# Four modulation-weight loads in another pool, and the scale and shift of turned norms on two engines

## The chip, the cores and the metric

The kernel runs on one core of one Trainium2 chip. A core has five engines with instruction queues of their own: TensorE (PE, with a separate queue row PEld for the loading of the stationary operand), VectorE (DVE), ScalarE (ACT), GpSimd (POOL) and SyncE (SP), which here only issues DMA transfers. The metric is the device time of one execution in microseconds (us). Three runs of the kernel before gave 1665.51, 1665.57 and 1665.77 us.

## What is computed

Two transformer blocks on 256 tokens of width 1024, each with two layers, all in fp32. The change lies in the first block. Cut to what matters, one of its layers is

```python
sh1, sc1, g1, sh2, sc2, g2 = adaln(c, w_mod[l], b_mod[l])      # silu(c) @ w_mod + b_mod, six parts of 1024
h = modulate(rms_norm(x, norm1_g[l]), sh1, sc1)                # h * (1 + scale) + shift
q, k, v, up, ca, cb = project_inputs(h, w_in[l], ...)
attn = diff_attn_post(diff_attention(q, k_all, v_all, lam), subln_g[l], lambda_init)
mix = concatenate([attn, pool_mixer(up), conformer_conv(ca, cb)])
x = x + g1 * (mix @ w_out[l])
x = x + g2 * swiglu(modulate(rms_norm(x, norm2_g[l]), sh2, sc2), w_ffn_in[l], w_ffn_out[l])
```

In layer 0 a second stream of 256 tokens (ctx) goes through the same steps beside x, with its own modulation; in layer 1 only x does. `diff_attention` has 4 heads with two softmaxes each, of which the second is subtracted from the first.

## The kernel before, in words

Tokens lie in four tiles t of 128 (t = 0, 1 are x, t = 2, 3 are ctx). Every product of weights is made of three fp32r products of high and low parts: the weights come by DMA into a tile `raw` (or `wm`), L202 (ScalarE) casts the high part, L204 (VectorE) subtracts it to get the low part, and L156 issues the matmuls. Work is written as Python generators that are woven together; a scheduler then sets the order of each engine's queue, and a tile's first write waits until the last readers of the tile that had its place before are done. So which pool a tile comes from changes when its load may start, and with that the order that the scheduler gives.

The pools that matter: `A8` (12 places of 8 KB per partition, activations), `hl` (4 places of 8 KB, split weights), and in PSUM `acc` (4 banks), `aux` (3 banks) and `ob` (1 bank). All loads are issued by SP, and `dma` (L148) chains them, so that SP issues them in program order: a load that waits for its place holds up every load behind it.

Attention of layer 0 runs at about 130 to 235 us. `front` (L1297 to L1304) makes two score matmuls of 64 rows into two `acc` banks (tile `acc` in the queue's rows), takes the maximum (L1297, VectorE), its negative (L1298), the exponential with its sum (L1299, ScalarE, which frees the bank), and combines the two halves (L1302 to L1304). For t = 0, 1 there are 512 keys, for t = 2, 3 there are 256. `back` turns the result (L248, `transpose4`, into `aux`), copies it (L1313, ScalarE) and multiplies it with the values into `ob`; `norm` (L1323 to L1329) scales, and `turn` (L1334, L1335) writes the operand of the output projection, whose matmuls are the first `acc<-hl,a` rows with 512 columns behind the attention.

Woven into it at two steps per step is `side()`: mixing and convolution, and then `ada_rows` for parts 2, 3 and 4 of the modulation: per part and half n two loads of 1 MB (`wm`, 12 loads in all) and eight matmuls of 32 rows by 512 columns per bank (`aux<-wm,csf`, 4 of them per load, each two records in the trace), then a copy (L341). Part 2 goes to the gates (L391), parts 3 and 4 to columns (matmuls with 2 columns, `aux<-km,s` 128x2, and L368).

The norms ahead of a layer's projections: `half_square` (L409), `halves_rstd` (L421, L422, GpSimd), the scaling in `norm_front` (L443, VectorE), and `norm_back`: four transposes into one `aux` bank, per column j one ScalarE activation with the tile's scale and shift (L461), the cast of the high part (L462, ScalarE) and the difference (L463, VectorE). It runs with scale and shift 10 times: for four tokens' tiles behind the output projection of layer 0 (266 to 293 us), for four ahead of layer 1 (653 to 680 us) and for two behind the output projection of layer 1 (797 to 820 us). Each time takes 8 columns, so L461 has 80 instructions.

Of the kernel before, what the change touches and what calls it, by code (L numbers as in the profile page):

```python
# [9 lines left out]
F32 = mybir.dt.float32  # L10
# [3 lines left out]
AF = mybir.ActivationFunctionType  # L14
ALU = mybir.AluOpType
# [4 lines left out]
P = 128  # L20
# [77 lines left out]
class _Kernel:  # L98
# [227 lines left out]
            k = k0 + j  # L326
            self.mm(o[j * GROUP:(j + 1) * GROUP, :], self.csf[:, k, :], raw[:, j, :], start=(k < 4), stop=(k >= 4))

    def ada_rows(self, l, part):
        out = []  # L330
        for n in range(2):
            c0 = part * D + n * 512
            b = self.bank()
            for k0 in range(0, KD, 4):
                raw = self.whl.tile([P, 4, 512], F32, tag="hl", name=self.nm("wm_"))
                self.dma(raw, self.wview(self.io["w_mod"][l], k0, 4, c0, c0 + 512))
                self.ada_products(b, k0, raw)
                if k0 == 0:
                    yield
            r = self.S2([P, 512])  # L340
            self.nc.vector.tensor_copy(r, b)  # L341
            out.append(r)
            yield
        self._rows = out
# [101 lines left out]
    def norm_back(self, x, t, G, S, out, halves=(0, 1)):  # L446

        nc = self.nc
        i = t * P
        for h in halves:  # L450
            b = self.transpose4([x[:, (4 * h + j) * P:(4 * h + j + 1) * P] for j in range(4)])
            hi, lo = (out[q][h][:, :, i:i + P] for q in range(2))
            tmp = self.S2([P, 4, P])
            if S is None:
                g = G(t)[:, 4 * h:4 * h + 4]
                nc.vector.tensor_mul(tmp, b, g.unsqueeze(2).to_broadcast([P, 4, P]))
            else:
                for j in range(4):
                    k = 4 * h + j
                    g, s = G(t)[:, k:k + 1], S(t)[:, k:k + 1]  # L460
                    nc.scalar.activation(tmp[:, j, :], b[:, j, :], AF.Identity, scale=g, bias=s)  # L461
            nc.scalar.copy(hi, tmp)  # L462
            nc.vector.tensor_sub(lo, tmp, hi.bitcast(F32))  # L463

# [487 lines left out]
    def layer1(self, l, S, xin, hT, first=()):  # L952

        nc, io = self.nc, self.io
# [16 lines left out]
        def band_load():  # L971
            band = self.A8([P, 2, 4, SEQ])
            for kt in range(2):
                self.dma(band[:, kt], io["k_band"][kt].rearrange("p (g t) -> p g t", g=4))
            return band
# [38 lines left out]
        def add(gts):  # L1014
            last = [None]

            def evac(t, n, b):
                cs = slice(n * 512, (n + 1) * 512)
                tmp = self.S2([P, 512])
                with self.behind(last[0]):  # L1020
                    nc.vector.tensor_mul(tmp, b, gts[t // 2][:, cs])
                r = res[t // 2][:, t % 2, cs]
                last[0] = nc.vector.tensor_add(r, r, tmp)  # L1023
                return last[0]
            return evac

        hT2 = None
        if not last:
            gates = [self.gate(l, 2, s) for s in streams]

            band, pp = band_load(), pool_pieces()

            def side():
                for s in streams:
                    for _ in self.pool_mix(S, stat, s, band, mB, pp):
                        next(conv, None)
                        yield
                mA.extend(self.parts(TQ))
                for _ in conv:
                    yield  # L1040
                yield from self.ada_rows(l, 2)
                self.rows_to_gates(gates)
                for p, d in ((3, 2), (4, 3)):
                    yield from self.ada_rows(l, p)
                    self.rows_to_cols(S.mod[:, d], S.part(p))

            rf = lambda t: res[t // 2][:, t % 2, :]
            out = self.out_proj(mstat, io["w_out"][l], TQ, add(gates), lambda t: done(t))

            def side_all():  # L1050
                yield from side()
                while not self.fronts:
                    yield
                for _ in range(2):
                    next(out)
                    yield

            self.weave(self.diff_attention(S, qT, kT, v, rq, q_toks, mA, LAG), side_all(), 2.0)
            for s, name in enumerate(("x", "ctx")):
                res[s] = self.reload(name)  # L1060
            G2, S2 = self.modulation(S, l, 1, "n2")
            hT2 = self.norm_out(512)
            done = self.norm_step(rf, G2, S2, hT2)
            for _ in out:
                pass
            g2, nxt = [None, None], []

            def side2():
                yield
                yield  # L1070
                for s in streams:
                    g2[s] = self.gate(l, 5, s)
                nxt.append(self.setup1(l + 1))
                yield from self.ada_sums(l, 5, streams)
                self.sums_to_gates(g2)
                nx = nxt[0]
                nx.rest()
                yield from self.setup2()
                self.gate_next = self.gate(l + 1, 2, 2)
                for p, d, st in ((0, 0, [0, 1]), (1, 1, [0, 1]), (3, 2, [0]), (4, 3, [0])):  # L1080
                    yield from self.ada_sums(l + 1, p, st)
                    self.sums_to_cols(nx.mod[:, d], nx.part(p))
                yield from self.ada_sums(l + 1, 2, [0])
                self.sums_to_gates([self.gate_next])

            end = {}

            def done_ffn(t):
                if t == 0:
                    end["hT"] = self.norm_out(512)  # L1090
                    end["step"] = self.norm_step(rf, *self.modulation(nxt[0], l + 1, 0, "n1"), end["hT"])
                end["step"](t)

            self.weave(
                self.ffn_wide(hT2, io["w_ffn_in"][l], io["w_ffn_out"][l], self.glu(512), add(g2), done_ffn),
                side2(), 0.85)
            return nxt[0], res[0], end["hT"]
# [24 lines left out]
        bias, nxt, end = [], [], {}  # L1122
# [687 lines left out]
```

## Time and profile before

| | before |
|---|---|
| median of 3 runs | 1665.57 us (1665.51 to 1665.77) |
| profiled execution | 1667.61 us |
| its span | 1665.8 us |
| mean granted TensorE clock | 0.983 |
| PE busy | 1618.0 us (97%) |
| DVE busy | 1180.4 us (71%) |
| ACT busy | 793.9 us (48%) |
| POOL busy | 43.8 us (3%) |

The span is what the trace covers; 1.8 us lie around it. The profiled execution took 2.04 us longer than the median. Busy shares are means over stages with different limits. The granted clock is given as a share of full speed: 1.00 is 2.4 GHz and 0.50 is 1.2 GHz, and a value between them is a mixture within the stretch.

### The profile page before, as it was taken

How to read it: one execution, taken by the hardware profiler on the slowest of the kernel's cores; microseconds unless marked ns; L12 is line 12 of the kernel's file. 1: busy time of each engine (PE TensorE's matmuls, PEld its weight loads, DVE VectorE, ACT ScalarE, POOL GpSimd, SP SyncE). 2: the span in 40 equal slices, each digit the busy share in tenths (PEclk: the TensorE clock that was granted, in tenths of full speed). 3: DMA queues.
4: the chain of work that ended last, by engine and by line, in shares of the span. 5: the costliest groups of instructions: out<-in, count | busy, mean ns of one | idle time of the engine just before them, and what ended most of it. 6: DMA issues, size and time to landing. Idle time of an engine off the chain costs nothing.

```text
span 1665.8 us, 24269 instructions
## 1 busy us (share of the span) xinstructions
PE 1618.0 (97%) x9241; PEld 1354.8 (81%) x9241; DVE 1180.4 (71%) x2130; ACT 793.9 (48%) x1347; POOL 43.8 (3%) x99
## 2 busy tenths in 40 slices
PE   7999999999999999999799899999999999999999
PEld 5787568878888888886698899767999987689998
DVE  4796656856575555986566457877887888778786
ACT  4334436323222224655543346765555577665554
POOL 1000000000000000000000001000000010000000
PEclk8999979999999999999899999999999999999999
DMA  9421651745375553432369655432656554246553
GB/s 329 129 89 59 245 177 55 225 148 168 108 228 174 175 153 113 140 114 82 99 224 243 194 188 159 151 102 88 204 181 190 177 150 150 87 128 189 189 181 122
DMA packets 183011, 262.71 MB, mean 158 GB/s; under 512 B 11277, under 2 KB 122864, under 8 KB 182896
## 3 DMA queue, kind: packets, MB, share of 16 engines
q1 hardware_dynamic: 182616, 260.85, 50.1%
q8 instruction: 72, 1.18, 0.3%
q10 hardware_dynamic: 280, 0.33, 0.2%
q14 instruction: 43, 0.35, 0.1%
HBM read 259.84 MB, written 1.31 MB: 157 GB/s over the span
## 4 chain that ended last, share of the span: by engine, by line
PE 69%; DVE 12%; issue 8%; DMA 6%; ACT 3%; POOL 1%; SPq 0%; POOLq 0%; ACTq 0%; DVEq 0%
PE aux L156 34%; PE acc L156 27%; PE ob L156 6%; DVE hl L204 3%; DMA raw<-in_w_mod_dram 3%; PE aux L248 2%; DVE a L1236 2%; DVE s L1236 1%; ACT hl L202 1%; DMA a<-dbias 1%; DMA raw<-in_w_ffn_out_dram 1%; DVE s L355 1%; DMA raw<-in_w_in_dram 1%; ACT s L461 1%; DVE sm L843 1%
## 5 line engine op out<-in xcount | busy, mean ns | idle before, releaser
L156 PE MATMUL acc<-hl,a 128*128 128x512 f32 (+3 forms) x3072 | 720.4, 387 | 8.1 <-ACT hl L202 2.9
L156 PEld LDWEIGHTS acc<-hl,a 128*128 128x128 f32 x3072 | 553.5, 190 | 127.2 <-issue 15.5
L202 ACT CAST hl<-raw 128x1024 fp32r<-128x1024 f32 (+2 forms) x382 | 393.6, 1036 | 473.5 <-PE aux L156 141.4
L156 PE MATMUL aux<-a,hl 128*128 128x256 f32 (+1 forms) x4032 | 578.5, 304 | 8.1 <-ACT a L462 2.9
L156 PEld LDWEIGHTS aux<-a,hl 128*128 128x128 f32 x4032 | 539.4, 192 | 41.5 <-ACT a L462 3.7
L204 DVE TENSOR_TENSOR hl<-raw,hl 128x1024 fp32r<-128x1024 f32 (+2 forms) x382 | 457.8, 1203 | 162.0 <-ACT hl L202 160.3
L355 DVE SCALAR_TENSOR_TENSOR s<-raw,csf,s 128x1024 f32<-128x1024 f32 x70 | 88.7, 1281 | 46.8 <-DMA raw<-in_w_mod_dram 46.7
L248 PEld LDWEIGHTS aux<-km,s 128*128 128x128 f32 (+1 forms) x384 | 45.2, 143 | 35.9 <-issue 20.1
L248 PE MATMUL aux<-km,s 128*128 128x128 f32 (+1 forms) x384 | 60.0, 284 | 12.3 <-DVE s L443 8.0
L156 PE MATMUL ob<-a,hl 128*128 128x512 f32 (+1 forms) x288 | 64.3, 372 | 0.0
L156 PEld LDWEIGHTS ob<-a,hl 128*128 128x128 f32 x288 | 51.2, 188 | 9.4
L524 ACT ACTIVATE s<-aux 128x512 f32<-128x512 f32 x33 | 19.7, 598 | 66.0 <-PE aux L156 66.0
L552 ACT ACTIVATE s<-s,c2a,c2b 128x256 f32<-128x256 f32 x88 | 48.0, 593 | 5.9 <-DVE s L549 5.9
L527 ACT CAST a<-s 128x512 fp32r<-128x512 f32 x33 | 20.4, 618 | 54.9 <-DVE s L526 54.8
L549 DVE TENSOR_TENSOR s<-aux,km 128x512 f32<-128x512 f32 x44 | 30.4, 691 | 20.5 <-PE aux L156 20.5
L1236 DVE SCALAR_TENSOR_TENSOR a<-up,c,a 128x512 f32<-128x512 f32 x60 | 43.5, 748 | 0.5
L525 DVE SCALAR_TENSOR_TENSOR s<-s,aux 128x512 f32<-128x512 f32 x33 | 22.6, 685 | 29.4 <-ACT s L524 29.4
L248 PE MATMUL aux<-km,a 128*128 128x128 f32 (+1 forms) x196 | 31.1, 289 | 10.5 <-ACT a L770 7.9
L409 ACT ACTIVATE jk<-a 128x512 bf16<-128x512 f32 x44 | 28.1, 640 | 25.2 <-DVE a L1023 19.7
L553 DVE SCALAR_TENSOR_TENSOR s<-s,c2a,s 128x255 f32<-128x255 f32 x88 | 38.7, 479 | 1.4 <-ACT s L552 1.4
L248 PEld LDWEIGHTS aux<-km,a 128*128 128x128 f32 (+1 forms) x196 | 23.7, 146 | 18.6 <-ACT a L770 8.1
L555 DVE SCALAR_TENSOR_TENSOR s<-s,c2b,s 128x255 f32<-128x255 f32 x88 | 38.7, 480 | 0.1
(257 smaller groups left out, 1364.3 us busy)
## 6 DMA issues: line engine op xcount, KB each, us to landing
raw<-in_w_ffn_in_dram SPq DMA_DIRECT2D x88, 512.0 KB
raw<-in_w_up_dram SPq DMA_DIRECT2D x88, 512.0 KB
raw<-in_w_in_dram SPq DMA_DIRECT2D x60, 512.0 KB
raw<-in_w_mod_dram SPq DMA_DIRECT2D x56, 512.0 KB
raw<-in_w_ffn_out_dram SPq DMA_DIRECT2D x44, 512.0 KB
raw<-in_w_down_dram SPq DMA_DIRECT2D x44, 512.0 KB
wm<-in_w_mod_dram SPq DMA_DIRECT2D x16, 1024.0 KB
raw<-in_w_out_dram SPq DMA_DIRECT2D x32, 512.0 KB
```

The source lines that it names most:

```text
L156: self.nc.tensor.matmul(o, lhsT, rhs, start=start, stop=stop)
L202: nc.scalar.copy(hl[:, 0, :n], raw[:, :n])
L204: nc.vector.tensor_sub(hl[:, 1, :n], raw[:, :n], hl[:, 0, :n].bitcast(F32))
L248: self.nc.tensor.transpose(b[:rows, j * P:(j + 1) * P], s, self.ident)
L355: self.nc.vector.scalar_tensor_tensor(accs[s], raw, c, accs[s], op0=ALU.mult, op1=ALU.add)
L409: self.nc.scalar.activation(junk, x[:, h * 512:(h + 1) * 512], AF.Square, scale=D ** -0.5, accum_out=ss[:, h:h + 1])
L525: nc.vector.scalar_tensor_tensor(th, th, 1.0, g, op0=ALU.add, op1=ALU.mult)
L549: nc.vector.tensor_mul(y, x.rearrange("p (j t) -> p j t", j=2), R2)
L552: nc.scalar.activation(o[:, j, :], y[:, j, :], AF.Identity, scale=wc(1, ff), bias=bc(ff))
L553: nc.vector.scalar_tensor_tensor(o[:, j, 1:SEQ], y[:, j, 0:SEQ - 1], wc(0, ff), o[:, j, 1:SEQ], op0=ALU.mult, op1=ALU.add)
L555: nc.vector.scalar_tensor_tensor(o[:, j, 0:SEQ - 1], y[:, j, 1:SEQ], wc(2, ff), o[:, j, 0:SEQ - 1], op0=ALU.mult, op1=ALU.add)
L1236: nc.vector.scalar_tensor_tensor(o, up[:, ct, :, k:k + SEQ], w, o, op0=ALU.mult, op1=ALU.add)
```

## The change

Two edits. In `ada_rows`, the two loads of half n = 1 of parts 2 and 3 of layer 0 take their places in `A8` and no longer in `hl`. In `norm_back`, the columns with odd j go to VectorE as one `tensor_scalar` (multiply by the scale, add the shift) that reads the same PSUM bank.

```diff
-    def ada_rows(self, l, part):
+    def ada_rows(self, l, part, more=False):
+
         out = []
         for n in range(2):
             c0 = part * D + n * 512
             b = self.bank()
             for k0 in range(0, KD, 4):
-                raw = self.whl.tile([P, 4, 512], F32, tag="hl", name=self.nm("wm_"))
+                if more and n:
+                    raw = self.A8([P, 4, 512])
+                else:
+                    raw = self.whl.tile([P, 4, 512], F32, tag="hl", name=self.nm("wm_"))
                 self.dma(raw, self.wview(self.io["w_mod"][l], k0, 4, c0, c0 + 512))
...
                     g, s = G(t)[:, k:k + 1], S(t)[:, k:k + 1]
-                    nc.scalar.activation(tmp[:, j, :], b[:, j, :], AF.Identity, scale=g, bias=s)
+                    if j % 2:
+                        nc.vector.tensor_scalar(tmp[:, j, :], b[:, j, :], g, s, op0=ALU.mult, op1=ALU.add)
+                    else:
+                        nc.scalar.activation(tmp[:, j, :], b[:, j, :], AF.Identity, scale=g, bias=s)
             nc.scalar.copy(hi, tmp)
             nc.vector.tensor_sub(lo, tmp, hi.bitcast(F32))
...
-                yield from self.ada_rows(l, 2)
+                yield from self.ada_rows(l, 2, True)
                 self.rows_to_gates(gates)
                 for p, d in ((3, 2), (4, 3)):
-                    yield from self.ada_rows(l, p)
+                    yield from self.ada_rows(l, p, p == 3)
                     self.rows_to_cols(S.mod[:, d], S.part(p))
```

SP's queue has the same 541 rows in the same order; four of the 12 `wm` loads have another destination. The scheduler gives the other engines another order in the attention. Lines behind the first edit have numbers higher by 4 in the changed kernel, and those behind the second by 7 (L461 is L468, and the new VectorE instruction is L466).

Place 1, TensorE in the attention of layer 0, where fronts of t = 2 (`acc_1658` to `acc_1774`, 64 rows, a pair each) stand beside modulation products (`aux_1638`, from the loads `wm_1639` and `wm_1645`). Before:

```order
L156 MATMUL acc_1607<-a_95_619,a_94_618 128x512
L156 MATMUL acc_1612<-a_95_619,a_94_618 128x512
L248 MATMUL aux_1620<-km,s_241_1537 128x128 x4
L248 MATMUL aux_1627<-km,s_235_1511 128x128 x4
L156 MATMUL aux_1638<-wm_1639,csf 32x512
L156 MATMUL ob_1574<-a_145_995,s_271_1632 128x128 x4
L156 MATMUL aux_1638<-wm_1639,csf 32x512 x3
L156 MATMUL aux_1638<-wm_1645,csf 32x512 x4
L156 MATMUL acc_1658<-a_95_619,a_94_618 128x256
L156 MATMUL acc_1663<-a_95_619,a_94_618 128x256
```

And in the changed kernel:

```order
L248 MATMUL aux_1627<-km,s_235_1511 128x128 x4
L156 MATMUL acc_1658<-a_95_619,a_94_618 128x256
L156 MATMUL acc_1663<-a_95_619,a_94_618 128x256
L156 MATMUL ob_1574<-a_145_995,s_271_1632 128x128 x4
L156 MATMUL acc_1713<-a_95_619,a_94_618 128x256
L156 MATMUL acc_1718<-a_95_619,a_94_618 128x256
L156 MATMUL acc_1769<-a_95_619,a_94_618 128x256
L156 MATMUL acc_1774<-a_95_619,a_94_618 128x256
L156 MATMUL aux_1638<-a_273_1639,csf 32x512 x4
L248 MATMUL aux_1671<-km,s_251_1560 128x128 x4
```

The three pairs `acc_1658`, `acc_1713` and `acc_1769` now stand together, ahead of the products of `aux_1638`, which before stood ahead of the first of them.

Place 2, VectorE in the changed kernel, some 20 instructions later in the same stage (L345 copies modulation rows, L395 adds to the gates, L372 adds to the columns, L1304 is the maximum of a front):

```order
L395 TENSOR_TENSOR gate_1161<-gate_1161,aux_1691 128x512
L345 COPY s_292_1707<-aux_1694 128x512
L1331 TENSOR_TENSOR s_302_1738<-ob_1574,sm_1739 128x512
L1334 TENSOR_REDUCE sm_1740<-s_301_1737 128x4
L372 TENSOR_TENSOR mod_535<-aux_1790,cb_590 128x8
L1304 TENSOR_REDUCE sm_1765<-acc_1769 128x1
L1336 TENSOR_TENSOR s_302_1738<-s_302_1738,sm_1746 128x512
L1305 SCALAR_TENSOR_TENSOR sm_1766<-sm_1765,rq_620 128x1
L1304 TENSOR_REDUCE sm_1765<-acc_1774 128x1
```

The maxima of the pair `acc_1769`, `acc_1774`, whose matmuls moved ahead, still stand behind L372, which needs matmuls (`aux_1790`) that come 18 rows later on TensorE.

Place 3, VectorE in the changed kernel at the norm behind the output projection of layer 1, second tile of tokens (L447 is the scaling, L466 the new instruction, `s_1094` and `s_1096` the two halves of 512):

```order
L447 TENSOR_SCALAR s_1087_6494<-a_400_2082,sm_6501 128x512 x2
L204 TENSOR_TENSOR hl_6599<-raw_6597,hl_6599 128x1024
L204 TENSOR_TENSOR hl_6628<-raw_6626,hl_6628 128x1024
L466 TENSOR_SCALAR s_1094_6511<-aux_6506,G_5998,S_5999 128x128
L466 TENSOR_SCALAR s_1096_6523<-aux_6518,G_5998,S_5999 128x128
L466 TENSOR_SCALAR s_1094_6511<-aux_6506,G_5998,S_5999 128x128
L466 TENSOR_SCALAR s_1096_6523<-aux_6518,G_5998,S_5999 128x128
L470 TENSOR_TENSOR a_1062_6367<-s_1094_6511,a_1061_6366 128x4x128
```

Two low parts of weights (L204) now stand between the scaling and the first odd column, and the columns of the two halves alternate, where on ScalarE the four columns of one half stood ahead of those of the other.

## Rows read from the trace of the kernel before

**Rows 1.** The page: busy time of each engine, and the chain that ended last.

```profile
PE 1618.0 (97%) x9241; PEld 1354.8 (81%) x9241; DVE 1180.4 (71%) x2130; ACT 793.9 (48%) x1347; POOL 43.8 (3%) x99
...
PE 69%; DVE 12%; issue 8%; DMA 6%; ACT 3%; POOL 1%; SPq 0%; POOLq 0%; ACTq 0%; DVEq 0%
```

**Rows 2.** Windows of the attention: length, busy of PE, PEld, DVE, ACT, POOL, clock, DMA, GB/s.

```profile
130.00:140.00 10.00, 8.19 (x32) 5.11 (x31) 9.89 (x19) 5.31 (x10) 0.00 (x0) 0.83 0.33 105
...
156.00:160.00 4.00, 4.00 (x23) 4.00 (x23) 2.05 (x8) 0.25 (x1) 1.22 (x2) 0.57 0.00 0
160.00:188.00 28.00, 27.98 (x170) 18.21 (x171) 18.35 (x44) 18.04 (x40) 1.52 (x3) 1.00 0.44 151
188.00:214.00 26.00, 25.23 (x164) 12.53 (x157) 15.95 (x52) 8.30 (x25) 1.20 (x2) 1.00 0.92 332
214.00:230.00 16.00, 12.98 (x44) 7.80 (x45) 8.74 (x26) 6.24 (x16) 1.20 (x2) 0.52 0.53 184
230.00:235.00 5.00, 5.00 (x17) 4.23 (x16) 3.85 (x13) 4.50 (x11) 0.00 (x0) 0.50 0.00 0
```

**Rows 3.** Waits of PE, then of SP's queue, 130 to 240 and 100 to 240.

```profile
PE aux L248 <- DVE s L1329: 2.0, 1, 2.0
PE acc L156 <- ACT s L1299: 1.7, 2, 1.0
...
SPq L148 <- PE aux L156: 31.3, 8, 12.9
```

**Rows 4.** Timeline of PE: start, duration, instruction, records, and idle time before.

```profile
184.05 1.09 PE L248 MATMUL aux<-km,s 128*128 128x128 f32 x8
185.08 1.04 PE L156 MATMUL aux<-wm,csf 128*32 128x512 f32 x2
186.05 1.16 PE L156 MATMUL ob<-a,s 128*128 128x128 f32 x8
187.14 1.92 PE L156 MATMUL aux<-wm,csf 128*32 128x512 f32 x14
188.99 0.70 PE L156 MATMUL acc<-a,a 64*128 64x256 f32 x4
...
214.38 1.03 PE L156 MATMUL acc<-a,a 64*128 64x256 f32 x2 [0.96 <-ACT s L1299]
...
226.00 1.22 PE L156 MATMUL ob<-a,s 128*128 128x128 f32 x4 [0.62 <-ACT s L1313]
...
230.44 3.33 PE L156 MATMUL acc<-hl,a 128*128 128x512 f32 x7
```

**Rows 5.** Timelines of ACT and DVE: the exponentials and maxima of fronts, and L368.

```profile
187.27 0.78 ACT L1299 ACTIVATE s<-acc,sm,rq 128x512 f32<-128x512 f32 x1 [0.46 <-DVE sm L1298]
...
190.85 0.57 ACT L1299 ACTIVATE s<-acc,sm,rq 128x256 f32<-128x256 f32 x1
...
186.43 0.74 DVE L1304 SCALAR_TENSOR_TENSOR s<-s,sm 128x512 f32<-128x512 f32 x1
...
204.45 0.17 DVE L368 TENSOR_TENSOR mod<-aux,cb 128x8 f32<-128x8 f32 x1 [0.73 <-PE aux L156]
204.53 0.41 DVE L1297 TENSOR_REDUCE sm<-acc 128x1 f32<-128x256 f32 x1
204.86 0.68 DVE L1329 TENSOR_TENSOR s<-s,sm 128x512 f32<-128x512 f32 x1
205.46 0.15 DVE L1298 SCALAR_TENSOR_TENSOR sm<-sm,rq 128x1 f32<-128x1 f32 x1
```

**Rows 6.** Groups by line: the activation that moves, and the nearest VectorE instructions.

```profile
L461 ACT ACTIVATE s<-aux,S,G x80: 448/466/520, 269.4 to 815.8; 128x128 f32<-128x128 f32 x80
...
L1260 DVE TENSOR_SCALAR s<-km,sm x6: 282/283/288, 158.7 to 744.0; 128x128 f32<-128x128 f32 x6
...
L779 DVE TENSOR_SCALAR a<-a,G,S x16: 405/411/416, 28.2 to 53.1; 128x256 f32<-128x256 f32 x16
```

**Rows 7.** Windows of the two norms of four tiles, columns as in rows 2.

```profile
270.00:290.00 20.00, 18.76 (x111) 15.94 (x111) 12.21 (x20) 18.73 (x46) 2.60 (x6) 1.00 0.18 58
...
680.00:738.00 58.00, 57.95 (x299) 48.92 (x297) 56.88 (x126) 25.90 (x39) 0.00 (x0) 1.00 0.44 137
```

**Rows 8.** Timeline of the norm behind the output projection of layer 1: PE, DVE, ACT.

```profile
811.70 1.94 PE L248 MATMUL aux<-km,s 128*128 128x128 f32 x8 [6.34 <-DVE s L443]
815.24 7.00 PE L156 MATMUL aux<-a,hl 128*128 128x256 f32 x42 [1.60 <-ACT a L462]
...
811.86 1.22 DVE L204 TENSOR_TENSOR hl<-raw,hl 128x1024 fp32r<-128x1024 f32 x1
...
812.83 1.86 ACT L461 ACTIVATE s<-aux,S,G 128x128 f32<-128x128 f32 x5 [2.91 <-PE aux L248]
814.55 0.64 ACT L462 CAST a<-s 128x512 fp32r<-128x512 f32 x1
```

**Rows 9.** Timeline of PE in the first FFN, where it waits for modulation sums.

```profile
506.04 2.34 PE L156 MATMUL aux<-a,hl 128*128 128x512 f32 x9 [1.60 <-DVE s L525]
```

## The prediction, made before the changed kernel ran

> **What bounds the kernel now.** I read the page first. TensorE is busy for 97% of the span, VectorE for 71%, ScalarE for 48%, and the chain that ended last lies on PE for 69% [rows 1]. So time is won or lost only where PE stands still or runs at the lower clock, and the change is judged at the places it touches: the attention of layer 0 and the three norms. The windows of the attention come next [rows 2]. Between 160 and 214 PE is busy for 53.2 of 54 us at the full granted clock. From 214 to 230 it is busy for 12.98 of 16 us at a clock of 0.52, and from 230 to 235 it works all the time at 0.50. So the end of this stage, not its middle, is what is slow before. The waits [rows 3] tell why loads matter little here: SP waits 31.3 us for modulation products to free its places, but no wait of PE in this stage ends on a DMA. PE waits 1.7 us for exponentials and 2.0 us for the scaling behind the last `ob`.
>
> **Earlier loads, priced alone: nothing.** The four loads bring the same bytes in the same order. Their first readers never waited for them, so their being there sooner ends no wait of PE. What they change is the order that the scheduler gives, and there lies the cost.
>
> **The first new wait, +2.8.** In the changed order three pairs of fronts stand together, with no modulation products between them. There are four `acc` banks, so the third pair waits for the exponentials of the first. I place it on the clock of before. The transposes that stand ahead of the moved pair end at 185.1 [rows 4]; one pair is 0.70 and the `ob` products 1.16, so PE reaches the second pair at about 186.9. VectorE takes the maximum of the first pair only behind a reciprocal that needs the sum of an earlier exponential, and that one runs from 187.27 to 188.05 [rows 5]. From there 0.41 (maximum), 0.15 and 0.57 (exponential) give the third pair's first bank at about 189.4; its second bank needs another 0.41, a 0.74 (L1304) that stands between, 0.15 and 0.57, and comes at about 191. From 186.9 to 191.3 are 4.4 us, in which PE has two pairs of work, 1.4, so 3.0 stand idle. Before, 14 records of products (1.92) and more filled this place [rows 4]. If ScalarE and VectorE, given the fronts earlier, run ahead where they have gaps, 1.4 are left. I take 2.8, near the chain as ordered, with 1.4 and 3.0 as ends.
>
> **The second, +1.5.** The maxima of `acc_1769` and `acc_1774` stand behind L372, which needs products that stand 18 rows later. From its inputs it takes 0.17, then 0.41, then 0.68 (L1336, which is now ahead of L1305 as L1329 was before), 0.15 and 0.57 until the bank is free for the next front [rows 5]: 2.0. Only one load's products lie ahead of that front on PE; 14 records take 1.92 [rows 4], so its eight cover some 0.5 at least. That leaves 1.5; ends 0.8 and 2.2, the latter if the second half follows in series. Queued behind these waits on PE are all later products of the stage.
>
> **Given back, -1.6.** The two waits late in the stage, 0.96 for an exponential at 214.38 and 0.62 for a copy at 226.00 [rows 4], should go, since the last fronts are now ahead of the last load's products. The 2.0 us wait at the end [rows 3] stays: the same chain of scaling stands behind the last `ob`. Ends -1.6 and 0.
>
> **The clock, +1.7.** The stretches 130 to 140 and 156 to 160 have clocks of 0.83 and 0.57 [rows 2], so each lost 1.7 us of full speed (10 x 0.17 and 4 x 0.43). Ahead of the first, PE did short fronts with waits of a microsecond or less. The two new waits put the same pattern into a stretch that ran at 1.00. I take one such fall; ends 0 and 3.4. [...]
>
> **The odd columns.** 40 of the 80 activations of 466 ns leave ScalarE. On VectorE the new operation is not in the trace; a tensor_scalar of the same shape from SBUF takes 283 ns, one with two scalars and twice the columns 411 ns [rows 6]. I take 0.28, nearest in shape; ends 0.17 (L368 with eight columns [rows 5]) and 0.41. So VectorE gains 11 us and ScalarE loses 18.6 of busy time, less in pitch: five activations in a row take 1.86 [rows 8], that is 0.35 each behind the first. In the changed order an odd column waits for the even one ahead of it in the same bank, so a half is no chain of four pipelined activations (0.47 + 3 x 0.35 = 1.5) but 2 x 0.47 + 2 x 0.28 = 1.5 with handoffs on top. So a half gets no shorter. The Trainium skill ("PSUM — Partial Sum Buffer", Terms) speaks against this split in the same way: two engines may not be in one bank at once. Were the two halves of the columns taken side by side, a half would last about 0.8, and each norm with an exposed end would gain 0.7; the sum goes without that.
>
> - Norm behind the output projection of layer 0: ScalarE is busy for 18.73 of 20 us, PE stands idle for 1.24 [rows 7]. 16 activations leave, at 0.35 some 5.6 us, so most of that idle time can go: -1.0. Ends -1.2 and +0.5 (handoffs).
> - Norm ahead of layer 1: right behind it VectorE is busy for 56.88 of 58 us with convolution taps, while PE has dense work throughout [rows 7]. The 16 columns delay VectorE by 4.5 us; PE has to wait only where it needs the taps' result at the end. I take +0.3; ends 0 and +2.
> - Norm behind the output projection of layer 1: nothing covers it. PE waits 6.34 and 1.60 [rows 8]. Before, the transposes let ScalarE begin at 812.83 and PE goes on at 815.24. In the changed order two L204 of 1.22 stand between VectorE's scaling and the first odd column, the first of them from 811.86 on, so that begins at 814.3 at the earliest. Then come 0.28, two activations of the even columns (0.47 and 0.35), 0.28 and the cast of 0.64: 816.2. So +0.9; ends 0 and +2.
>
> **Absorbed, -0.8.** Behind the first norm PE waits 1.60 at 506 for VectorE [rows 9], on a chain of modulation loads that runs beside the FFN. A stage that ends later eats into that wait; I take half. Ends -1.6 and 0.
>
> **Sum.** +2.8 +1.5 -1.6 +1.7 for the attention, -1.0 +0.3 +0.9 for the norms, -0.8 absorbed: **+3.8 us**. The profiled execution took 1667.61, so 1671.4 by its measure; it is 2.04 above the median of the runs, and 1665.57 + 3.8 is **1669.4 us**. The own range of this case is 1666.5 to 1674: the lower end takes the attention's terms near their low ends, the upper one both falls of the clock and nothing given back. No change, as far as a measurement of this kernel can tell, is within 0.2%, that is 1662.2 to 1668.9; so the forecast is slower, but only just.
>
> **Rivals.**
> 1. The end of the attention loses its lower clock: faster. Before, the clock falls at 214 behind small matmuls and a wait of 0.96. In the changed order the last fronts come sooner and products of the last load stand behind them, so that the end is denser. For it: the 12.98 us of busy time at 0.52 [rows 2] would be 6.7 at full speed, 6.2 less. Against it: the last `ob` products, transposes and the 2.0 us wait stay. It decides if the clock is still 1.00 at the last products. Then the sum is 3.8 - 6.2 - 1.7 (no fall earlier either) = -4.1: **1661.5**. Chance 0.20.
> 2. The new waits hide: ScalarE and VectorE run ahead, the waits are 1.4 and 0.8, the clock holds. 0.6 for the attention, +0.2 for the norms, -0.8: **1665.6**, no change. For it: both engines are busy for only 18 of the 28 us from 160 to 188 [rows 2]. Against it: the order of VectorE's queue, which puts maxima behind things that PE makes later. Chance 0.25.
> 3. The change does not do what it says: the places in `A8` come free no sooner than those in `hl`, so nothing arrives earlier and PE meets products that wait for their loads. From 188 to 214 the DMA share is 0.92 [rows 2], so loads of 1 MB follow each other at some 3.2 us (at that window's 332 GB/s), and one that comes a place late is as much behind. Against it: in the order two of the four have the same releaser as the `hl` places or an earlier one. It would cost about as much as the first new wait: **1668**. Chance 0.07.
>
> **Chances.** The forecast has 0.48, 0.43 of it above 1668.9. Rival 1 is faster. Slower: 0.43. No change: 0.05 + 0.25 + 0.07 = 0.37. Faster: 0.20. The range for 8 in 10 reaches from 1661 (rival 1) to 1674.
>
> **What would show it.** Right: in the changed profile PE waits for L1306 (the exponential) near 187 to 191 and again some 17 us later, with a granted clock under 1.00 between; the waits at 214 and 226 are gone; the first matmul of the output projection begins 3 to 5 us after 230.44 [rows 4]; the first norm's idle time on PE is under 0.5; PE goes on behind the last norm about 5 us later than 815.24. Wrong: a window from 214 to the output projection at a clock near 1.00, or PE idle in the middle of the attention under 1 us in all.

## The result, and the profile after

The changed kernel takes 1675.01 us (median of 5 runs, 1672.88 to 1682.00) against 1665.57 us before (5 runs, 1665.14 to 1667.16). The ratio is 1.0059, 95% interval 1.0044 to 1.0073: **slower by 9.4 us**. Forecast were 3.8 us and a range up to 1674. The direction was right, the measured loss is 2.5 times the forecast. One execution of all the runs below, in experiment 5, took 2272 us at a granted clock of 0.65; it is left out of that experiment's ratio.

The profiled execution took 1675.28 us, with a span of 1672.6. First the page's busy times, the lines that answer to [rows 1].

```profile
PE 1620.6 (97%) x9241; PEld 1356.8 (81%) x9241; DVE 1193.4 (71%) x2170; ACT 782.5 (47%) x1307; POOL 44.9 (3%) x99
```

VectorE has 40 instructions and 13.0 us more, ScalarE 40 instructions and 11.4 us less. TensorE's work is the same. So the loss is time in which TensorE waits or runs slowly, and the waits of PE from 130 to 240 show the first part of it; they answer to [rows 3].

```profile
PE acc L156 <- ACT s L1306: 4.6, 6, 1.9
PE ob L156 <- ACT s L1320: 3.0, 4, 1.8
PE aux L248 <- DVE s L1336: 1.6, 1, 1.6
```

The kernel before had, beside the two lines of [rows 3]:

```profile
PE ob L156 <- ACT s L1313: 0.8, 2, 0.6
```

Waits of fronts for exponentials grew from 1.7 to 4.6 us, those of the `ob` products from 0.8 to 3.0 (a second profile of the kernel before, experiment 9, has 1.7 for the latter). The timeline of PE in the attention shows where (start, duration, instruction, records, idle time before); it answers to [rows 4].

```profile
187.44 0.70 PE L156 MATMUL acc<-a,a 64*128 64x256 f32 x2
188.52 0.70 PE L156 MATMUL acc<-a,a 64*128 64x256 f32 x2 [0.38 <-ACT s L1306]
189.98 0.70 PE L156 MATMUL acc<-a,a 64*128 64x256 f32 x2 [0.77 <-ACT s L1306]
190.99 0.83 PE L156 MATMUL acc<-a,a 64*128 64x256 f32 x2 [0.31 <-ACT s L1306]
191.75 1.94 PE L156 MATMUL aux<-a,csf 128*32 128x512 f32 x8
...
198.03 1.06 PE L156 MATMUL aux<-a,csf 128*32 128x512 f32 x8
...
211.54 1.77 PE L156 MATMUL acc<-a,a 64*128 64x256 f32 x4 [1.93 <-ACT s L1306]
...
232.66 1.22 PE L156 MATMUL ob<-a,s 128*128 128x128 f32 x4 [1.80 <-ACT s L1320]
235.51 1.54 PE L248 MATMUL aux<-km,s 128*128 128x128 f32 x6 [1.62 <-DVE s L1336]
236.70 3.02 PE L156 MATMUL acc<-hl,a 128*128 128x512 f32 x7
```

Three matmuls of fronts wait one behind the other at 188 to 191, a front at 211, and the output projection begins at 236.70, where it began at 230.44. The second part of the loss is in the windows of the same stage (columns as in [rows 2]).

```profile
190.00:196.00 6.00, 5.59 (x19) 2.22 (x20) 1.98 (x10) 1.56 (x5) 0.00 (x0) 0.72 0.00 1
196.00:211.00 15.00, 12.94 (x80) 5.60 (x79) 7.58 (x17) 2.15 (x6) 1.20 (x2) 1.00 0.46 147
211.00:219.00 8.00, 7.46 (x30) 4.72 (x30) 4.03 (x19) 2.60 (x10) 0.00 (x0) 0.57 1.03 401
219.00:232.00 13.00, 10.97 (x71) 5.97 (x70) 7.26 (x22) 6.06 (x15) 0.00 (x0) 1.00 0.19 69
232.00:239.00 7.00, 4.72 (x16) 3.94 (x17) 4.56 (x14) 3.01 (x9) 1.20 (x2) 0.53 0.46 150
```

The clock falls three times: at 191 and 212, each time at one of the new waits, and at 232. A fall at the end of the stage is in the kernel before, too (experiment 9), so the first two are the change's. The eight records of products at 191.75 take 1.94, where the eight at 198.03, at full speed, take 1.06.

### The profile page after: what moved, and what is told of

The parts are those of the page before. It is cut to its first block, busy times and chain, and to the rows that moved or that the text cites. A ratio compares the mean times of both kernels' runs of the same rounds, so it can differ in the third digit from the quotient of the medians.

```text
span 1672.6 us, 24259 instructions
## 1 busy us (share of the span) xinstructions
PE 1620.6 (97%) x9241; PEld 1356.8 (81%) x9241; DVE 1193.4 (71%) x2170; ACT 782.5 (47%) x1307; POOL 44.9 (3%) x99
## 4 chain that ended last, share of the span: by engine, by line
PE 71%; DVE 12%; DMA 6%; issue 6%; ACT 3%; POOL 1%; SPq 1%; ACTq 0%; DVEq 0%; POOLq 0%
PE aux L156 33%; PE acc L156 29%; PE ob L156 6%; DVE hl L204 3%; DMA raw<-in_w_mod_dram 3%; PE aux L248 3%; DVE a L1243 2%; ACT hl L202 1%; DVE s L1243 1%; DMA raw<-in_w_ffn_out_dram 1%; DVE s L359 1%; DMA raw<-in_w_ffn_in_dram 1%; DMA raw<-in_w_in_dram 1%; DMA raw<-in_w_up_dram 1%; SPq L148 1%
## 5 line engine op out<-in xcount | busy, mean ns | idle before, releaser
L204 DVE TENSOR_TENSOR hl<-raw,hl 128x1024 fp32r<-128x1024 f32 (+2 forms) x382 | 457.1, 1201 | 168.0 <-ACT hl L202 166.0
L248 PE MATMUL aux<-km,s 128*128 128x128 f32 (+1 forms) x384 | 59.9, 286 | 10.4 <-DVE s L447 6.6
L156 PEld LDWEIGHTS ob<-a,hl 128*128 128x128 f32 x288 | 51.2, 188 | 10.2 <-DVE hl L204 0.9
L556 DVE TENSOR_TENSOR s<-aux,km 128x512 f32<-128x512 f32 x44 | 30.3, 690 | 20.5 <-PE aux L156 20.5
```

What stands on the lines that cost most here:

```text
L156: self.nc.tensor.matmul(o, lhsT, rhs, start=start, stop=stop)
L204: nc.vector.tensor_sub(hl[:, 1, :n], raw[:, :n], hl[:, 0, :n].bitcast(F32))
L248: self.nc.tensor.transpose(b[:rows, j * P:(j + 1) * P], s, self.ident)
L556: nc.vector.tensor_mul(y, x.rearrange("p (j t) -> p j t", j=2), R2)
```

## The experiments

Eleven experiments ran: nine other kernels, and the two of this case once more. The table gives medians, the ratio to runs of the kernel before on the same chip with its 95% interval, and three numbers of each profile. "Stage" is the time from the first front of layer 0 to the first matmul of its output projection, "idle" what PE waited in it from 30 us on, and "at 1.2 GHz" the sum of 2 x (1 - granted clock) over windows of 1 us from there to 14 us into the output projection. A profile is one execution and need not be like the median: that of experiment 3 is of its fastest execution (1672.96 us), that of experiment 4 of its slowest (1668.70).

| kernel | median, us | ratio (95%) | stage | idle | at 1.2 GHz |
|---|---|---|---|---|---|
| before (profile of 1667.61) | 1665.57 | | 99.4 | 3.8 | 20.5 |
| the change | 1675.01 | 1.0059 (1.0044 to 1.0073) | 105.5 | 8.6 | 17.1 |
| 1 norms alone | 1666.15 | 1.0003 (0.9993 to 1.0012) | 97.1 | 5.2 | 10.2 |
| 2 four loads alone | 1678.67 | 1.0068 (1.0048 to 1.0087) | 112.0 | 7.9 | 37.6 |
| 3 part 2 alone | 1677.66 | 1.0063 (1.0050 to 1.0076) | 105.0 | 8.7 | 17.0 |
| 4 part 3 alone | 1663.44 | 0.9986 (0.9975 to 0.9997) | 95.6 | 3.6 | 10.4 |
| 5 fronts held | 1666.59 | 0.9997 (0.9988 to 1.0006) | 95.6 | 5.5 | 6.9 |
| 6 scaling late | 1675.53 | 1.0053 (1.0039 to 1.0067) | 103.6 | 6.8 | 20.5 |
| 7 parts 3 and 4 | 1664.25 | 0.9979 (0.9970 to 0.9988) | 94.2 | 3.5 | 6.8 |
| 8 part 3, four-tile norms | 1662.58 | 0.9978 (0.9969 to 0.9988) | 93.6 | 3.7 | 6.8 |
| 9 before again | 1663.94 (one run) | | 95.9 | 5.2 | 6.8 |
| 10 the change again | 1675.73 (one run) | | 105.4 | 8.5 | 17.0 |
| 11 parts 3 and 4, four-tile norms | 1664.25 | 0.9989 (0.9980 to 0.9998) | 95.6 | 3.5 | 10.4 |

Take from each stage its idle time and half of its time at 1.2 GHz, and 85.3 to 88.4 us are left in all thirteen rows, while the stages themselves lie between 93.6 and 112.0. (With the time at 1.2 GHz inside the stage alone it is 86.5 to 89.8.) So these two terms carry most of the difference between the stages.

**Experiments 1 to 4: which part.** Theories: A, the order of TensorE in the attention; B, the split norms; C, the early loads or their places. Experiment 1 is the kernel before with the second edit alone, experiment 2 with the first alone, experiments 3 and 4 with a part of the first. (The cuts show the lines against the changed kernel; the second edit is taken back in both.)

```diff
 experiment 3
-                    yield from self.ada_rows(l, p, p == 3)
+                    yield from self.ada_rows(l, p)
 experiment 4
-                yield from self.ada_rows(l, 2, True)
+                yield from self.ada_rows(l, 2)
```

> The norm split alone, all modulation loads as before. Theory A (the loss is the order of TensorE in the attention): -2 to +1 us against the kernel before; PE's wait of 0.37 and 0.78 in the first norm goes, the last norm's wait of 1.60 on the cast grows to about 2.5. Rival B (the split norms cost, too): +2 to +5 us. Rival C (early loads or the places in A8 cost): -2 to +1, as A.

Measured: no difference (1.0003). B falls, its lower end of +2 us just at the end of the interval.

> The four loads in A8 alone, norms as before. A and C: +7 to +11 us, as much as the whole change or a little more; output projection of layer 0 begins some 6 us late, with waits of PE for exponentials near 188 to 191 and 211. B: +3 to +6.

Measured: 1.0068, the whole loss. Its profile has nearly the waits of the changed kernel, 4.3 and 2.7 us, and yet it is 6.5 us longer in the stage. Waits, timeline and the last window of that profile:

```profile
PE acc L156 <- ACT s L1303: 4.3, 6, 1.9
PE ob L156 <- ACT s L1317: 2.7, 3, 1.8
```

```profile
243.89 1.63 PE L156 MATMUL acc<-hl,a 128*128 128x512 f32 x3
```

```profile
211.00:246.00 35.00, 30.41 (x115) 18.69 (x116) 16.28 (x55) 11.64 (x32) 1.20 (x2) 0.52 0.42 153
```

Here the clock falls at 211, at the same wait of 1.9 us, and stays low to the output projection; in the profile of the change it came back at 219. This order's executions lie from 1671.74 to 1683.67; that the length of the second fall makes this spread fits, but only one of them was profiled.

> Only the two loads of part 2 go to A8; the queue of TensorE is the same as with all four. A: the same loss as the four loads, within 2 us. C: about half of it, since only half of the places and early transfers are left.

Measured: 1.0063. The two loads of part 2 alone give the loss, with the queue of TensorE that they bring: in the traces of experiments 2 and 3, TensorE, VectorE and ScalarE have the same order in this stage as in the changed kernel. Part 2's own loads do not even start sooner. SP's queue before, then in the changed kernel:

```profile
163.94 25.54 SPq L148 DMA_DIRECT2D wm<-in_w_mod_dram  x6
```

```profile
164.28 3.13 SPq L148 DMA_DIRECT2D a<-in_w_mod_dram  x2
168.56 3.61 SPq L148 DMA_DIRECT2D a<-in_w_mod_dram  x2
```

The two of part 2 are the first in each fence, at 163.94 and 164.28; only the loads behind them come sooner. Those of part 3 in `A8` are issued from 168.56 on, where before they were the last two of six that took until 189.48. Why the scheduler moves the fronts ahead for the places of part 2, no run shows.

> Only the two loads of part 3 go to A8; TensorE keeps nearly the order of the kernel before, the fronts stay behind their products. A: within 2 us of the kernel before, either way, no wait for exponentials of over 1 us. C: +3 to +5, the other half.

Measured: 0.9986, a little faster than the kernel before. The same kind of load in the same pool costs nothing where the order stays, so C falls. Waits of PE in its profile, from 130 to 245:

```profile
PE ob L156 <- ACT s L1317: 1.1, 1, 1.1
PE acc L156 <- ACT s L1303: 0.7, 1, 0.7
```

Fronts wait 0.7 here. TensorE's order is nearly that of the kernel before. The last products, which are due sooner with these loads, stand a few places ahead of where they stood before.

**Experiment 5: the loads of the change, the fronts held.** The whole change; only the first three pairs of fronts of t = 2 may not pass the products that stand ahead of them in the program.

```diff
-            self.mm(o[j * GROUP:(j + 1) * GROUP, :], self.csf[:, k, :], raw[:, j, :], ...)
+            self.adam = self.nc.tensor.matmul(o[j * GROUP:(j + 1) * GROUP, :], self.csf[:, k, :], raw[:, j, :], ...)
...
-                self.mm(sb[:, :nk * P], ...)
+                with self.behind(self.adam if t == 2 and h < 3 else None):
+                    self.mm(sb[:, :nk * P], ...)
```

> The whole change, all four loads early in A8, but the first three pairs of fronts of t = 2 are held on TensorE behind the modulation products ahead of them in the program, as in the kernel before. Order is the cost: the loss goes, -4 to +3 us against the kernel before. The early loads or their places are the cost: it stays at +7 to +11.

Measured: 0.9997. The loss is gone, with SP issuing the loads as in the changed kernel. Timeline of PE and two windows of its profile:

```profile
187.82 1.16 PE L156 MATMUL ob<-a,s 128*128 128x128 f32 x8 [0.87 <-ACT s L1322]
210.69 0.70 PE L156 MATMUL acc<-a,a 64*128 64x256 f32 x2 [0.47 <-ACT s L1308]
```

```profile
188.00:214.00 26.00, 25.53 (x164) 12.41 (x164) 18.49 (x56) 10.10 (x29) 1.20 (x2) 1.00 0.66 244
214.00:224.00 10.00, 7.51 (x53) 4.46 (x52) 6.38 (x19) 5.02 (x12) 0.00 (x0) 1.00 0.18 63
```

From 188 on no wait of a front is over half a microsecond, and the clock is 1.00 from 188 to 224. Theory A holds: the order is the cost. VectorE and ScalarE get another order with the fronts held, too, so it is the order of all three queues; that of TensorE alone was not separated.

**Experiment 6: the second wait.** The timeline of the changed kernel's VectorE and ScalarE ahead of 211.54 shows another gate than the one that I had named:

```profile
208.66 0.17 DVE L372 TENSOR_TENSOR mod<-aux,cb 128x8 f32<-128x8 f32 x1
208.74 0.41 DVE L1304 TENSOR_REDUCE sm<-acc 128x1 f32<-128x256 f32 x1
209.98 0.69 DVE L1336 TENSOR_TENSOR s<-s,sm 128x512 f32<-128x512 f32 x1 [0.83 <-POOL sm L163]
210.59 0.15 DVE L1305 SCALAR_TENSOR_TENSOR sm<-sm,rq 128x1 f32<-128x1 f32 x1
...
210.84 0.56 ACT L1306 ACTIVATE s<-acc,sm,rq 128x256 f32<-128x256 f32 x1 [2.98 <-DVE sm L1305]
```

The maximum does stand right behind L372, but L372 itself does not wait; the scaling L1336, between a front's maximum and its negative, waits 0.83 for GpSimd. The experiment puts it behind the maxima:

```diff
-            nc.vector.tensor_mul(on, on, rs.unsqueeze(2).to_broadcast([P, HN, P]))
             def turn():
+                with self.behind(self.neg):
+                    nc.vector.tensor_mul(on, on, rs.unsqueeze(2).to_broadcast([P, HN, P]))
```

where `self.neg` is the last front's L1305.

> The whole change with the order of fronts that it gives, but VectorE's scaling of the finished tokens (L1336), which waits for GpSimd between the two maxima of a front, is put behind the maxima. If that, and not L372, makes the second new wait: the wait of 1.9 us near 209 to 211 falls under 0.6 and the clock falls there more seldom, +2 to +7 us against the kernel before. If L372 makes it: no change to the whole change, +8 to +11.

Measured: 1.0053, no time back, so the time lies where it was expected if L372 made the wait. The wait itself says otherwise. Timeline of PE in its profile:

```profile
187.49 0.70 PE L156 MATMUL acc<-a,a 64*128 64x256 f32 x2 [1.50 <-ACT s L1306]
...
211.98 1.49 PE L156 MATMUL acc<-a,a 64*128 64x256 f32 x4 [0.74 <-ACT s L1306]
```

The wait fell from 1.93 to 0.74, though not under 0.6, as it had to if L1336 made most of it; the rest is the chain of maximum, negative and exponential behind L372. But the run does not price this wait, for the edit changed more. TensorE's order moved again: another wait of 1.50 stands at 187, and the clock falls at 189 and 212 all the same (20.5 us at 1.2 GHz). And the scaling is in layer 1 as well, where PE now waits for it (its line is L1339 in this kernel):

```profile
792.13 0.84 PE L248 MATMUL aux<-km,s 128*128 128x128 f32 x4 [1.51 <-DVE s L1339]
```

The clock is 0.89 from 785 to 800, where the changed kernel had 1.00 from 780 to 796. With the wait that is some 3 us (an estimate, 1.51 + 15 x 0.11) lost outside of the stage. What the second wait alone is worth stays open.

**Experiments 7, 8 and 11: what the change is good for.** Part 2 stays in `hl` in all three. Experiment 7 has parts 3 and 4 in `A8`, norms as before; experiment 8 part 3, with the split norms where there are four tiles of tokens; experiment 11 both.

```diff
 experiments 8 and 11
-                    if j % 2:
+                    if j % 2 and out[0][0].shape[-1] > 256:
```

> The second halves of parts 3 and 4 go to A8, part 2 stays, norms as before; TensorE keeps the order of the run with part 3 alone. If the gain of part 3 alone comes from loads that are there when the last products are due: as fast as that run or up to 2 us faster, -2 to -5 us. If it comes from the order alone: the same, -2 to -3.

> Part 3 alone in A8, and the norm split kept for the two norms of four tiles, taken back for the last norm of two tiles. Each was worth about: part 3 -2.3, the split 0, the last norm +0.4 in the profile. So -1.5 to -4 us against the kernel before.

> Parts 3 and 4 in A8, part 2 not, the norm split for the two norms of four tiles alone: what the runs so far found no loss in. 0 to 2 us faster than the best of the two runs with these parts, so -3 to -6 us against the kernel before, if the parts add; -2 to -3 if the first FFN's wait for modulation sums takes the rest.

Measured: 0.9979, 0.9978 and 0.9989, that is -3.5, -3.7 and -1.8 us. All are faster than the kernel before, 11 only just (its interval ends at 0.9998) and by less than either of its two expectations, and far faster than the change. The intervals of 7 and 8 do not tell them from each other or from part 3 alone, and the parts do not add. One place takes part of the gain back in some executions: near 500, in the first FFN, PE waits for modulation sums 1.9, 2.1 and 1.3 us in the profiles of 4, 5 and 7, but 0.3 and 0.7 in those of 8 and 11, and 1.6 and 0.4 in the two of the kernel before. Experiment 8 has the lowest median, 1662.58 us. Two windows of its profile:

```profile
188.00:214.00 26.00, 26.00 (x168) 12.95 (x162) 17.00 (x55) 9.99 (x28) 1.20 (x2) 1.00 1.04 390
214.00:220.00 6.00, 4.86 (x33) 3.36 (x30) 5.26 (x15) 3.67 (x9) 0.00 (x0) 1.00 0.15 48
```

PE is never idle from 188 to 214, and the clock holds up to 220.

**Experiments 9 and 10: both kernels again.**

> The kernel before, profiled once more, for the clock in its attention. If its usual execution has less of the lower clock than the profile that the sum was read from (20 us behind 214): some 10 us at 1.2 GHz between 160 and the output projection, which begins 1 to 3 us sooner, span 1663 to 1665. If that profile was typical: 18 to 22 us again, span 1665 to 1667.

> The changed kernel, profiled once more. TensorE's waits in the attention are the same as in the first profile (8 to 9 us from 160 on) whatever the time; what varies is the time at 1.2 GHz, 17 us or 30 to 40, and the output projection begins some 105 or some 112 us behind the first front accordingly. If the waits vary instead, they differ by over 2 us.

Measured: the kernel before has 6.8 us at 1.2 GHz in this profile, not 20.5, though its waits are not smaller. Windows and waits of that profile:

```profile
188.00:214.00 26.00, 25.81 (x168) 12.67 (x163) 15.84 (x49) 8.70 (x24) 1.20 (x2) 1.00 0.90 324
214.00:224.00 10.00, 6.95 (x42) 4.09 (x40) 7.98 (x26) 6.02 (x14) 0.09 (x1) 1.00 0.76 272
224.00:232.00 8.00, 6.02 (x20) 5.20 (x21) 5.53 (x19) 5.14 (x12) 1.11 (x2) 0.57 0.22 68
```

```profile
PE aux L248 <- DVE s L1329: 2.5, 1, 2.5
PE ob L156 <- ACT s L1313: 1.7, 2, 1.5
PE acc L156 <- ACT s L1299: 1.7, 2, 1.0
```

Here the clock does not fall behind 214, where it did in the profile of [rows 2], at the same instructions; the wait of 0.96 for an exponential is there in both. So the profile that the prediction was read from held 14 us of lower clock that this execution does not have. Half of that is 7 us, but the stage was only 3.5 us longer: PE at full speed waits 1.4 us more, and the rest is not accounted for. The usual execution lies between the two. Of 66 executions of the kernel before that ran beside the experiments, 9 took as long as the first profile's 1667.61 us or longer, and 3 were faster than this one; their median granted clock is 0.986, against 0.983 and 0.988 in the two profiles. The change, profiled again, has the same waits (8.5 us) and the same 17 us at 1.2 GHz as the first time; the 37.6 of experiment 2 is another pattern of the same order. Over all thirteen profiles: in the five where the fronts moved ahead (the change, 2, 3, 6 and 10) the clock falls between 189 and 193 and again near 212 or 213, in the other eight at neither place.

## Why the prediction was right or wrong, point by point

- **Earlier loads alone: nothing.** Right, as far as experiment 5 goes (0.9997). But the two loads of part 2, which bring the loss, start no sooner at all (164.28 against 163.94). Where TensorE's order stays (experiment 4) they gain a little, 0.14%, which the sum did not have.
- **First new wait, +2.8 (1.4 to 3.0).** Right in place, kind and size, though the idle times alone, 0.38 + 0.77 + 0.31 = 1.46, look like the low end. Matmuls of a pair that wait one by one take 0.70 each in the profile, where an undisturbed pair takes 0.70 in all [rows 4]. From 187.44 to 191.75 PE does two pairs of work, 1.4 us, in 4.31: 2.9 us are lost. The second pair waits, too, not only the third, and PE came 0.5 us later to it than I had it.
- **Second new wait, +1.5 (0.8 to 2.2).** It measured 1.93, within the ends, in part by luck. The order was read rightly, since the maximum starts at 208.74 right behind L372. But in the chain behind it L1336 waits 0.83 for GpSimd, which I did not have, while the products ahead cover 1.0 us and not 0.5.
- **Given back, -1.6.** Failed. Waits of the same kinds stay late in the stage: fronts wait another 0.47 at 220.19, `ob` products 0.68 and 1.80. PE's idle time in the stage grew by 4.8 us against the first profile and by 3.4 against the second, where my three terms made 2.7. Part of what I hoped to get back was small only because PE ran slowly: the wait of 0.62 at 226.00 [rows 4] is 1.54 in experiment 9, at the full clock.
- **The clock, +1.7 for one fall (0 to 3.4).** This is the step that failed most. The mechanism was named, its size was not. Two falls come with the new waits, at 191 and 212. In both profiles of the change they last 10 us together (in experiment 2 some 37), and half of that, up to 5.1 us, is lost where 1.7 was forecast. Against experiment 1, whose old order has a fall of its own near 206, it is 3.4 us. The second error is the baseline. The profile of before held 20.5 us at 1.2 GHz, more than the change's 17.1, so against that profile the clock term is not a loss at all. I had seen that its execution was 2.04 us over the median, and put the sum on the median without asking where these 2 us lay.
- **The sum of the stage.** 105.5 against 95.9 and 97.1 (experiments 9 and 1) is 8.4 to 9.6 us, against the first profile's 99.4 it is 6.1; I had 4.4. The spans differ by 10.4 and 9.3, and by 6.8, so some 0.8 us of the loss lie outside of the stage, where -0.6 (norms and absorption) was forecast.
- **The odd columns.** 0.28 was taken for one, from the row of the same shape; they measure 0.402, near the row with two scalars (0.41). In pitch it is less: the 40 add 13.0 us to VectorE's busy time, 0.33 each.

```profile
L466 DVE TENSOR_SCALAR s<-aux,G,S x40: 396/402/410, 275.5 to 818.2; 128x128 f32<-128x128 f32 x40
```

- **The norms, -1.0 +0.3 +0.9.** Together 0.2 was forecast, experiment 1 has 1.0003 (-0.0007 to +0.0012, that is -1.2 to +2.0 us). In the profile of the change, PE's waits of 0.37 and 0.78 in the first norm became one of 0.67, so half a microsecond came back, not 1.0. In the last norm the order did what it was read to do:

```profile
814.46 1.94 PE L248 MATMUL aux<-km,s 128*128 128x128 f32 x8 [5.77 <-DVE s L447]
818.94 21.24 PE L156 MATMUL aux<-a,hl 128*128 128x256 f32 x159 [2.54 <-ACT a L469]
```

```profile
814.62 2.35 DVE L204 TENSOR_TENSOR hl<-raw,hl 128x1024 fp32r<-128x1024 f32 x2
816.89 0.72 DVE L466 TENSOR_SCALAR s<-aux,G,S 128x128 f32<-128x128 f32 x2
```

The two L204 hold up the first odd columns to 816.89, and the wait for the cast grew by 0.94 to 2.54 ([rows 8] has 1.60). The wait ahead of it shrank by 0.57, so the norm lost 0.4, not 0.9. (The steps of the forecast add up to 816.3 and +1.1, not 816.2 and +0.9.) In the norm ahead of layer 1 PE's waits grew from 0.4 to 0.9.
- **Absorbed, -0.8.** PE's wait of 1.60 near 506 [rows 9] is gone in the profile of the change, so all of it was taken there. In the second profile of the kernel before that wait is only 0.44, so in such an execution there is little to absorb.
- **Rivals.** Rival 1 asked the right question, whether the clock holds at the end of the stage, and had the sign wrong for this order: it falls sooner. The clock did hold longer in the kernel before itself (experiment 9) and in experiments 7 and 8. Rival 2 fell with the two waits. Of rival 3 the condition held for the two loads of part 2, which start no sooner, but not its cost: PE waited for no load.
- **The signs.** The waits for L1306 came at 188 to 191 and some 20 us later. But waits late in the stage stayed, the output projection began 6.3 us after 230.44 and not 3 to 5, the first norm's wait was 0.67 and not under 0.5, and PE went on behind the last norm 3.7 us later and not 5.

Open: what decides whether the clock comes back after 219 or stays low to the output projection; the waits ahead of it are nearly the same in both cases. Nor is a wait alone enough to bring a fall: the 0.96 ahead of a front in experiment 9 and the 0.87 at 187.82 in experiment 5 brought none. Nor is one needed: from 156 to 160 PE is busy all the time, at 0.57 [rows 2]. The Trainium skill ("TensorE: Matmul & The Clock Gate", Part 1) says that the gate looks at activity in a window that runs free of the kernel, so that the point at which the clock changes differs between executions. The two profiles of the kernel before agree in that the point differs (behind 214 in one, behind 224 in the other); that they also differ in how long the clock stays low, 20.5 and 6.8 us, and that the window is the reason, no run explains. Three things were not tried: the order of the change with the loads at their old times, the order of TensorE changed without that of VectorE and ScalarE, and work put into the new waits to hold the clock.

## What to carry to other kernels

A load that moves to another pool can cost nothing itself and time still be lost, because the scheduler gives the engines another order, here even where the load started no sooner: compare the queues first, and look for consumers of a small ring of buffers that now stand together without other work between them. In a stretch of small matmuls count a new wait twice, for its length and for the clock that may fall with it, and measure what is lost from the first instruction to the last, since idle time shows only part of it. And before a profile becomes the baseline, ask what its own execution had: if it lies off the median, find the stretch where, or profile it again.

## What was not expected of the hardware

The clock's lower stretch at the same place of the same program came and went between executions: 20.5 and 6.8 us in two profiles of the kernel before, 17.1, 17.0, 17.0 and 37.6 in four of the changed order (with and without the split norms). A VectorE tensor_scalar of 128 columns took 402 ns from PSUM with two scalars per partition, against 283 ns for one of that shape with one scalar from SBUF [rows 6].
